# Layer 0 attention with two heads' scores in two row halves of the array and one exponential for both, and linear attention issued between groups of value products

## The chip, the cores and the metric

The kernel runs on one core of one Trainium2 chip. The metric is the time of one execution in microseconds of the device; three runs of the kernel before gave a median of 3662.07 us (3659.19 to 3665.93). The engines are named as in the profile: PE (TensorE, the matrix array; PEld are its weight loads), DVE (VectorE), ACT (ScalarE), POOL (GpSimd) and SP (SyncE, which issues most of the transfers). Each engine takes its own instructions in the order in which they were written to it, and waits on semaphores for the others. All arithmetic is in 32 bits; A matmul of F32R operands is one instruction of the array, one of plain F32 operands is two (L914 is written 592 times and stands 1184 times in the profile); products in F32R are made exact enough by splitting an operand into a high and a low part.

## What is computed

Two layers over 2048 latent tokens with 256 context tokens ahead of them, so T = 2304 rows in 18 tiles of 128. Layer 0 has two mixers side by side, latent attention (8 heads, 96 numbers in a query or key, of which 64 without and 32 with rotary positions, 64 in a value) and bidirectional gated linear attention (4 heads); layer 1 is neighbourhood attention. The part that matters here, cut from the reference:

```python
def block_attention(q, k, v, scale):
    ...
    def one(qi):
        s = jnp.einsum('bqhd,bkhd->bhqk', qi, k, preferred_element_type=jnp.float32) * scale
        p = jax.nn.softmax(s, axis=-1).astype(v.dtype)
        return jnp.einsum('bhqk,bkhd->bqhd', p, v)
    ...
def gla_scan(q, k, v, g, s0):
    ...
    def step(state, inp):
        qi, ki, vi, gi = inp
        b = jnp.cumsum(gi, axis=-2)
        b_last = b[..., -1:, :]
        q_t = qi * jnp.exp(b)
        k_t = ki * jnp.exp(-b)
        att = jnp.where(mask, jnp.einsum('bhld,bhmd->bhlm', q_t, k_t), 0.0)
        o = jnp.einsum('bhld,bhde->bhle', q_t, state) + jnp.einsum('bhlm,bhme->bhle', att, vi)
        k_dec = ki * jnp.exp(b_last - b)
        state = state * jnp.exp(b_last)[..., 0, :, None] + jnp.einsum('bhld,bhle->bhde', k_dec, vi)
        return state, o
```

Latent queries attend to all 2304 keys, context queries to the 256 context keys. The linear attention runs forward and backward over the rows, context first.

## The kernel before

The program is written with a framework that places each engine's instructions by dependencies and by the order of the text, and hoists work that is ready; `tc.issue_after(x)` adds an edge that keeps what is traced inside it behind `x` on `x`'s engine. What lies around the change:

**Latent stage** (`even_latent`). For each tile of rows `fin` turns queries and keys to one column per row, splits them into high and low and stores them to the scratch tensors `QT` and `KT`, [head, part, 97, T]: rows 0 to 95 the numbers, row 96 of the high part of `KT` ones. `even_rest` makes the remaining projections; its `maxes` takes the largest score of each row from the high parts and stores its negative as row 96 of `QT`, so that the scores come out with the maximum taken off.

**Attention** (`even_attention`). Heads go in four pairs `j`. For each pair there are five query blocks `nb`: 256 context queries against two key tiles, then four blocks of 512 latent queries against 18 key tiles. For each key tile and head three matmuls add up in one PSUM bank `st`: high keys by high queries (L972, 97 rows with the maximum), high keys by low queries (L973) and low keys by high queries (L974). ACT takes the exponential into `apt` and DVE adds it to `acc`, one instruction each per head. Value products are queued in `pend`; whenever six key tiles stand there, four are issued (`tail`, L914), each head into its own column half of one bank `av`, in plain F32. Two key tiles after a block's last value product `end` calls `finish`: column sums of `acc` into the bank `den` (L846), logarithm, exponential, the division and the gate on POOL, and the store to `RT`. PSUM holds three `st` banks, one `den`, two `av` and two `gl`.

**Linear attention** (`gla`). It is called once after the attention's first step, so its text stands ahead of nearly all of the attention's, and the framework fills in scores and values where it waits. For each of 18 chunks `front` makes the logits (L720), the logarithm of the sigmoid on ACT, cumulative sums (L731) and sums by halves (L735) and the decayed queries and keys; `back` transposes them (L758), multiplies within the chunk (L768, 64 rows each, forward and backward directions in the two row halves of the array), then by the values (L777, L783). After all chunks come two scans (forward on POOL, backward on DVE) and, in backward order, the read (L822) and write (L834). All of it shares the two `gl` banks.

**Around both** (`even_mix`). After the linear attention's text come 16 loads and splits of the output weights into places that the linear attention has left, then the remaining attention; `project` follows.

Of the kernel before, what the change touches and what calls it, by code (L numbers as in the profile page):

```python
# [17 lines left out]
P = 128  # L18
# [70 lines left out]
class Kern:  # L89
# [311 lines left out]
    def even_latent(self, ws, wrest, kept):  # L401
        nc, tc = self.nc, self.tc
        self.QT = self.scr("QT", (A_HEADS, 2, A_QK + 1, T), F32)
        self.KT = self.scr("KT", (A_HEADS, 2, A_QK + 1, T), F32)
        self.Vn = self.scr("Vn", (P, NT, 512), F32)
        self.Un = self.scr("Un", (NT, P, 1568), F32)
        with ExitStack() as es:
# [34 lines left out]
            one = self.tl(sp, [P, Q_LORA], "sql", bufs=1)  # L442
            nc.gpsimd.memset(one[:8], 1.0)
            for o in range(0, T, Q_LORA):
                nc.sync.dma_start(self.KT[:, 0, A_QK, o : o + Q_LORA], one[:8])
# [104 lines left out]
            def fin(t):  # L550
                qn, kn = nat.pop(t)
                for z, (src, dst) in enumerate(((qn, self.QT), (kn, self.KT))):
                    col = 2 * z + (0 if t < NCT else 1)
                    for h2 in range(2):
                        ps = self.tl(pp, [P, 4, P], "tp")
                        for j in range(4):
# [6 lines left out]
                        nc.sync.dma_start(  # L563
                            dst[h2 * 4 : h2 * 4 + 4, :, :A_QK, t * P : t * P + P].rearrange("h s d t -> d (h s) t"),
                            hl[:A_QK].rearrange("d h s t -> d (h s) t").bitcast(F32))
# [42 lines left out]
    def even_rest(self, ws, win, hT):  # L608
        nc = self.nc
        self.zaT = self.scr("zaT", (4, P, T), F32)  # L610
        with ExitStack() as es:
# [33 lines left out]
            def maxes():  # L645
                for h in range(A_HEADS):
                    k = self.tl(sp, [P, T], "mk", F32R, bufs=2)
                    nc.sync.dma_start(k[:A_QK].bitcast(F32), self.KT[h, 0, :A_QK])
                    m = self.tl(sp, [P, NT, 5], "mm")
                    nc.vector.memset(m[:], -3e38)  # L650
                    for t in range(NT):
                        if t % 6 == 0:
                            q = self.tl(sp, [P, 768], "mq", F32R)
                            nc.sync.dma_start(q[:A_QK].bitcast(F32), self.QT[h, 0, :A_QK, t * P : t * P + 768])
# [13 lines left out]
                    nc.gpsimd.dma_start(self.QT[h, 0, A_QK].rearrange("(t p) -> t p", p=P), r[:NT].bitcast(F32))  # L668
# [9 lines left out]
    def gla(self, gp, gs, g1, gd, pp, tag):  # L678
# [25 lines left out]
        z4 = lambda a: a.rearrange("p (h z d) -> p h z d", z=2, h=H)  # L704

        def front(c):

            u = self.tl(g1, [P, 1056], "gu")
            nc.sync.dma_start(u[:], self.Un[c, :, :1056])
            gq, gk, gv = u[:, :256], u[:, 256:512], u[:, 512:1024]  # L710
            ps = bank()
            u3 = self.tl(gs, [P, 3, 32], "gu3")
            g.tensor_copy(u3[:], u[:, 1024:1056].unsqueeze(1).to_broadcast([P, 3, 32]))
# [4 lines left out]
            yield  # L718
            lg = bank()
            nc.tensor.matmul(lg[:], r[:], gw[:], start=True, stop=True)  # L720
# [5 lines left out]
            nc.vector.scalar_tensor_tensor(out=G[:], in0=lg[:], scalar=0.0, in1=e[:], op0=ALU.min, op1=ALU.subtract)  # L726
# [62 lines left out]
        for _ in front(0):  # L789
            pass  # L790
# [68 lines left out]
    def even_attention(self, ap, pp, ahead):  # L859
# [133 lines left out]
        while late:  # L993
            step_late()
# [742 lines left out]
```

## Time and profile before

| | |
|---|---|
| median of three runs | 3662.07 us (3659.19 to 3665.93) |
| span of the profiled execution | 3650.5 us |
| PE busy | 3552.0 us, 97% |
| DVE, ACT, POOL busy | 65%, 39%, 34% |
| latent stage | about 0 to 550 us |
| layer-0 attention with linear attention | 1093 to 1974 us |
| linear attention within it | to about 1880 us |

The page gives no time of its own for the profiled execution beside its span; the span runs from the first to the last instruction. A row of a group of instructions has line, engine, operation, tile written <- tiles read, shapes and count, then the busy time in us, the mean of one in ns, and the idle time of the engine just ahead of them with what ended it. A row of the order of time has start and length in us, then the same names; like instructions in a row are merged, and what stands in brackets is idle time and its cause. A row of a table of stretches has the stretch, its length, busy time and count of each engine, the clock granted to TensorE as a share of full, and the transfers' share. A row of waits has who waited for whom, the total in us, the times and the longest. Line 106 is the helper that issues every activation.

### The profile page before, as it was taken

To read this page: it belongs to the slowest core of one execution; us is meant where nothing else is said; L and a number is where in the kernel's file an instruction comes from. 1 tells how busy PE (TensorE), PEld (TensorE's weight loads), DVE (VectorE), ACT (ScalarE), POOL (GpSimd) and SP (SyncE) were. 2 spreads that over 40 slices of the span, in tenths; PEclk is the share of its full clock that TensorE was granted. 3 is DMA by queue.
4 is the path that set the end of the run, shared out by engine and by line. 5 is a ranking of instruction groups with operands and counts; after the bars stand their busy time and mean duration, and the time that the engine had idled before them with its cause. 6 is when DMAs were issued, how large, how long until landed. Compare 5 with 4: busy or idle time off the path is not lost. (4 is left out here: it accounts for less than half of the span.)

```text
span 3650.5 us, 51811 instructions
## 1 busy us (share of the span) xinstructions
PE 3552.0 (97%) x18404; PEld 2747.6 (75%) x18404; DVE 2355.2 (65%) x4846; ACT 1433.2 (39%) x2740; POOL 1234.9 (34%) x1376
## 2 busy tenths in 40 slices
PE   8999999999999999999999999999899999999899
PEld 6988987888886666665656887888788887555577
DVE  4677666888876766678765435455488784666732
ACT  5445551111115555555654214444422222555510
POOL 1433330101011211221311224333344442888763
PEclk9999999999999999999999999999999999999999
DMA  7455463222243232342632544545734446898672
GB/s 259 142 156 155 135 177 110 87 75 84 69 116 86 66 107 66 89 125 66 179 110 93 184 139 141 159 146 155 245 126 144 131 133 181 212 223 220 190 235 97
DMA packets 365780, 512.25 MB, mean 140 GB/s; under 512 B 26081, under 2 KB 245297, under 8 KB 359618
## 3 DMA queue, kind: packets, MB, share of 16 engines
q1 hardware_dynamic: 320754, 417.69, 39.3%
q0 software_dynamic: 22112, 63.26, 5.7%
q10 hardware_dynamic: 22656, 27.99, 2.2%
q8 instruction: 146, 2.39, 0.3%
q14 instruction: 112, 0.92, 0.1%
HBM read 329.45 MB, written 179.37 MB: 139 GB/s over the span
## 5 line engine op out<-in xcount | busy, mean ns | idle before, releaser
L963 DVE TENSOR_TENSOR acc<-acc,apt 128x512 f32<-128x512 f32 x512 | 375.6, 756 | 168.5 <-ACT apt L106 165.6
L106 ACT ACTIVATE apt<-st 128x512 f32<-128x512 f32 (+1 forms) x592 | 343.6, 594 | 290.7 <-PE st L974 262.0
L660 DVE TENSOR_REDUCE mm<-mx 128x1 f32<-128x512 f32 (+1 forms) x656 | 388.7, 629 | 87.3 <-PE mx L659 80.0
L914 PE MATMUL av<-apt,av 128*64 128x512 f32 (+1 forms) x1184 | 280.6, 594 | 0.0
L972 PE MATMUL st<-aq,akh 97*128 97x512 f32 (+1 forms) x592 | 256.6, 434 | 8.8 <-DMA aq<-QT 4.4
L659 PE MATMUL mx<-mk,mq 96*128 96x512 f32 (+1 forms) x656 | 235.8, 373 | 5.0 <-DMA mq<-QT 3.4
L1430 POOL TENSOR_TENSOR oacc<-oacc,opt 128x576 f32<-128x576 f32 (+5 forms) x192 | 223.0, 1184 | 39.7 <-ACT rl L106 19.3
L973 PE MATMUL st<-aq,akh 96*128 96x512 f32 (+1 forms) x592 | 235.5, 398 | 0.0
L1548 DVE TENSOR_TENSOR opt<-st,tab 128x64 f32<-128x64 f32 (+10 forms) x576 | 144.6, 317 | 140.3 <-PE st L1391 63.8
L974 PE MATMUL st<-aq,akl 96*128 96x512 f32 (+1 forms) x592 | 234.4, 396 | 0.0
L106 ACT ACTIVATE u<-gm 128x352 f32<-128x352 f32 (+1 forms) x140 | 68.6, 498 | 373.2 <-PE gm L131 210.6
L1307 DVE CUSTOM_DVE_ANT_1 mx<-mx,mtab 128x217 f32<-128x217 f32 (+12 forms) x576 | 184.2, 338 | 40.1 <-PE mx L1301 30.9
L914 PEld LDWEIGHTS av<-apt,av 128*64 128x64 f32 x1184 | 80.5, 137 | 153.6 <-issue 152.3
L972 PEld LDWEIGHTS st<-aq,akh 97*128 97x128 f32 x592 | 113.0, 191 | 99.1 <-issue 50.5
L106 ACT ACTIVATE opt<-opt 128x930 f32<-128x930 f32 (+7 forms) x129 | 104.2, 810 | 110.7 <-DVE opt L1548 102.6
L659 PEld LDWEIGHTS mx<-mk,mq 96*128 96x128 f32 x656 | 121.2, 188 | 16.8 <-DMA mk<-KT 3.8
L974 PEld LDWEIGHTS st<-aq,akl 96*128 96x128 f32 x592 | 113.9, 193 | 25.6
L973 PEld LDWEIGHTS st<-aq,akh 96*128 96x128 f32 x592 | 114.4, 193 | 17.1
L129 PE MATMUL gm<-w1h,hhi 128*128 128x512 f32 x288 | 116.3, 404 | 6.8 <-ACT onat L106 6.8
L106 ACT ACTIVATE x<-px,modB,modA 128x128 f32<-128x128 f32 x272 | 99.3, 468 | 56.9 <-PE px L339 54.4
L129 PE MATMUL gm<-w0h,hhi 128*128 128x512 f32 x288 | 116.3, 404 | 2.0 <-DVE hhi L351 1.9
L807 POOL TENSOR_TENSOR gsf<-gsf,D 64x512 f32<-64x512 f32 x17 | 25.1, 1477 | 271.4 <-DVE D L784 271.4
(492 smaller groups left out, 9962.1 us busy)
## 6 DMA issues: line engine op xcount, KB each, us to landing
q<-Q SPq DMA_DIRECT2D x48, 512.0 KB
H<-x ACTq DMA_DIRECT2D x36, 512.0 KB
adaw<-ada_w SPq DMA_DIRECT2D x64, 256.0 KB
x<-H SPq DMA_DIRECT2D x32, 512.0 KB
wraw<-w_od SPq DMA_DIRECT2D x64, 256.0 KB
K1t<-okt POOLq DMA_DIRECT2D x32, 512.0 KB, 7.6
kt<-K1t SPq DMA_DIRECT2D x32, 512.0 KB
mtab<-rpb_q SPq DMA_DIRECT2D x16, 899.0 KB
```

The costliest lines, as they stand in the source:

```text
L106: return self.nc.scalar.activation(out, in_, func, **kw)
L129: self.nc.tensor.matmul(out, lh(k), rh(k), start=j == 0, stop=False)
L659: mm = nc.tensor.matmul(ps[:, :w], q[:A_QK, (t % 6) * P : (t % 6) * P + P], k[:A_QK, k0 : k0 + w], start=True, stop=True)
L660: nc.vector.tensor_reduce(out=m[:, t, n : n + 1], in_=ps[:, :w], axis=AX.X, op=ALU.max)
L914: nc.tensor.matmul(O[j, nb][i * 64 : i * 64 + 64, :w], V[j, kt // TT][:, kt % TT, i * 64 : i * 64 + 64], pts[i][:, :w], start=n == 0, stop ...
L963: nc.vector.tensor_tensor(out=acc[i][:, :w], in0=a[:, :w], in1=pts[i][:, :w], op=ALU.add)
L972: nc.tensor.matmul(ps[:, :w], kh[: A_QK + 1, i, kq], qh[: A_QK + 1, :w], start=True, stop=False)
L973: nc.tensor.matmul(ps[:, :w], kh[:A_QK, i, kq], ql[:A_QK, :w], start=False, stop=False)
L974: mm = nc.tensor.matmul(ps[:, :w], kl[:A_QK, i, kq], qh[:A_QK, :w], start=False, stop=True)
L1307: nc.vector.tensor_tensor_reduce(out=s, in0=s, in1=tb[:, ri : ri + rn, ci : ci + cn], scale=1.0, scalar=-3e38, op0=ALU.add, op1=ALU.max, a ...
L1430: self.psum = nc.gpsimd.tensor_tensor(out=a, in0=a, in1=pts[:, :, a0 - r0 : a1 - r0, :], op=ALU.add)
L1548: bias = nc.vector.tensor_tensor(out=pt[:, d[0], d[1]], in0=ps[:, d[0], d[1]], in1=tabs[j][i][:, ri : ri + rn, ci : ci + cn], op=ALU.add)
```

## The change

Scores of two heads are made together. A score is split into 64 plain and 32 rotary numbers: scratch tensors are now `QA`, `KA` ([part, head, 64, T]), `QC`, `KC` ([head, part, 32, T]) and `QM` (the negative maxima). A key tile of a head pair has slot 0 with 64 plain numbers of one head in rows 0 to 63 and of the other in 64 to 127, and slot 1 with the rotary numbers (high ones twice in the high tile; the low ones with a row of ones in the low tile). Five terms take the place of three, each a matmul of one head in rows 0 to 63 and of the other in 64 to 127 of the array: plain high by high, high by low and low by high; rotary high keys by high and low queries at once; rotary low keys by high queries with the ones by the negative maximum (33 rows). They go to a `st` of two banks, of which there are two; one activation and one addition cover both heads. `den` is taken from the `gl` banks.

The linear attention becomes a generator of 128 steps (`low_rank`, `logits`, `decays`, `turn`, `within`, `values`, `scan`, `read`, `write`), followed by 16 steps of output weights. Where four value products are issued, one step is drawn ahead of them, behind the scores, and one behind them. The first two query blocks of the next head pair are loaded at the third key tile of the block before.

```diff
-        self.QT = self.scr("QT", (A_HEADS, 2, A_QK + 1, T), F32)
-        self.KT = self.scr("KT", (A_HEADS, 2, A_QK + 1, T), F32)
+        self.QA, self.KA = [self.scr(n, (2, A_HEADS, A_NOPE, T), F32) for n in ("QA", "KA")]
+        self.QC, self.KC = [self.scr(n, (A_HEADS, 2, A_ROPE, T), F32) for n in ("QC", "KC")]
+        self.QM = self.scr("QM", (A_HEADS, T), F32)
...
-                        nc.sync.dma_start(
-                            dst[h2 * 4 : h2 * 4 + 4, :, :A_QK, t * P : t * P + P].rearrange("h s d t -> d (h s) t"),
-                            hl[:A_QK].rearrange("d h s t -> d (h s) t").bitcast(F32))
+                        hs, ts = slice(h2 * 4, h2 * 4 + 4), slice(t * P, t * P + P)
+                        for part in range(2):
+                            nc.sync.dma_start(da[part, hs, :, ts].rearrange("h d t -> d h t"), hl[:A_NOPE, :, part, :].bitcast(F32))
+                        nc.sync.dma_start(dc[hs, :, :, ts].rearrange("h s d t -> d (h s) t"),
+                                          hl[A_NOPE:A_QK].rearrange("d h s t -> d (h s) t").bitcast(F32))
...
+        def scan(c, sl, eng, name):
...
+        low_rank(0)
+        yield
+        low_rank(1)
+        logits(0)
+        yield
+        for c in range(NT):
+            decays(c)
+            yield
+            if c + 2 < NT:
+                low_rank(c + 2)
+            if c + 1 < NT:
+                logits(c + 1)
+            yield
+            turn(c)
+            yield
+            within(c)
+            yield
+            values(c)
+            scan(c, slice(0, 64), nc.gpsimd, "gsf")
+            yield
+        order = self.back_order()
+        for n in range(NT + 1):
+            if n < NT:
+                scan(order[n], slice(64, 128), nc.vector, "gsb")
+                read(order[n])
+                yield
+            if n:
+                write(order[n - 1])
+                yield
...
+            for part in range(2):
+                dma(q[:, part, :w], self.QA[part, 2 * j : 2 * j + 2, :, qs].rearrange("h d t -> (h d) t"))
+            dma(q[:, 2, :w], self.QC[2 * j : 2 * j + 2, :, :, qs].rearrange("h s d t -> (h s d) t"))
+            for i in range(2):
+                dma(q[i * 64 : i * 64 + 32, 3, :w], self.QC[2 * j + i, 0, :, qs])
+            for i in range(2):
+                last = dma(q[i * 64 + 32 : i * 64 + 33, 3, :w], self.QM[2 * j + i : 2 * j + i + 1, qs])
...
-            self.finish(O.pop((j, nb))[:, :w], sums.pop((j, nb)), zt[:, :w], self.RT[j, :, q0 : q0 + w], w, ap, pp, ("den", 1))
+            self.finish(O.pop((j, nb))[:, :w], sums.pop((j, nb)), zt[:, :w], self.RT[j, :, q0 : q0 + w], w, ap, pp, ("gl", 2))
...
-                        ps = self.tl(pp, [P, 512], "st", bufs=3)
-                        nc.tensor.matmul(ps[:, :w], kh[: A_QK + 1, i, kq], qh[: A_QK + 1, :w], start=True, stop=False)
-                        nc.tensor.matmul(ps[:, :w], kh[:A_QK, i, kq], ql[:A_QK, :w], start=False, stop=False)
-                        mm = nc.tensor.matmul(ps[:, :w], kl[:A_QK, i, kq], qh[:A_QK, :w], start=False, stop=True)
-                        pt = self.tl(ap, [P, 512], "apt", bufs=14)
-                        self.act(pt[:, :w], ps[:, :w], AF.Exp, scale=A_SCALE)
+                    ps = self.tl(pp, [P, 2, 512], "st", bufs=2)
+                    terms = ((kh, 0, 0, 64), (kh, 0, 1, 64), (kl, 0, 0, 64), (kh, 1, 2, 64), (kl, 1, 3, 33))
+                    for m, (k, kb, qb, r) in enumerate(terms):
+                        for o in (0, 64):
+                            mm = nc.tensor.matmul(ps[:, o // 64, :w], k[o : o + r, kb, kq], Q[o : o + r, qb, :w], start=m == 0, stop=m == 4)
+                    pts = self.tl(ap, [P, 2, 512], "apt", bufs=7)
+                    self.act(pts[:, :, :w], ps[:, :, :w], AF.Exp, scale=A_SCALE)
...
                     with self.tc.issue_after(mm.ins):
                         step_late()
                         if len(pend) == 6:
+                            next(side, None)
                             for _ in range(4):
-                                tail(*pend.pop(0))
+                                mm = tail(*pend.pop(0))
+                            with self.tc.issue_after(mm.ins):
+                                next(side, None)
+                    if nb == 4 and j < 3:
+                        if n == 2:
+                            for b in range(2):
+                                early[b], _ = queries(j + 1, b)
```

240 lines of the change are left out of this document (123 added, 117 removed).

## The prediction

> **What bounds the kernel now.** I read the page's first lines, then the table of stretches for the layer-0 attention, then the groups of instructions in it.
>
> ```profile
> span 3650.5 us, 51811 instructions
> PE 3552.0 (97%) x18404; PEld 2747.6 (75%) x18404; DVE 2355.2 (65%) x4846; ACT 1433.2 (39%) x2740; POOL 1234.9 (34%) x1376
> core 0: us, PE busy (x) PEld busy (x) DVE busy (x) ACT busy (x) POOL busy (x), PEclk, DMA share, GB/s
> 1095.00:1975.00 880.00, 868.17 (x4223) 537.66 (x4224) 607.04 (x879) 479.42 (x957) 168.83 (x167) 0.99 0.33 93
> L914 PE MATMUL av<-apt,av 128*64 128x512 f32 x1152 | 276.2, 600 | 0.0
> L972 PE MATMUL st<-aq,akh 97*128 97x512 f32 x576 | 251.3, 436 | 7.5 <-DMA aq<-QT 4.4 <-ACT apt L106 3.0
> L973 PE MATMUL st<-aq,akh 96*128 96x512 f32 x576 | 231.1, 401 | 0.0
> L974 PE MATMUL st<-aq,akl 96*128 96x512 f32 x576 | 230.2, 400 | 0.0
> ```
>
> PE sets the end: 868 of 880 us in this stage. ACT and DVE are busy 54% and 69% of it. So only PE time, or a new PE wait, counts. A matmul's listed duration (0.40 us) overlaps its neighbours; its price is the distance from its start to the next start. I read that from the order of time near the end of the stage, where the linear attention is finished and only scores (L972 to L974) and value products (L914) run.
>
> ```profile
> 1903.42 0.40 PE L973 MATMUL st<-aq,akh 96*128 96x512 f32 x1
> 1903.42 0.19 PEld L974 LDWEIGHTS st<-aq,akl 96*128 96x128 f32 x1
> 1903.65 0.40 PE L974 MATMUL st<-aq,akl 96*128 96x512 f32 x1
> 1903.98 3.65 PE L914 MATMUL av<-apt,av 128*64 128x512 f32 x16
> 1904.89 0.14 PEld L914 LDWEIGHTS av<-apt,av 128*64 128x64 f32 x2 [0.29 <-issue]
> 1905.32 0.14 PEld L914 LDWEIGHTS av<-apt,av 128*64 128x64 f32 x2 [0.29 <-issue]
> 1907.56 0.50 PE L972 MATMUL st<-aq,akh 97*128 97x512 f32 x1
> 1907.90 0.39 PE L973 MATMUL st<-aq,akh 96*128 96x512 f32 x1
> 1908.14 0.40 PE L974 MATMUL st<-aq,akl 96*128 96x512 f32 x1
> 1908.37 0.40 PE L972 MATMUL st<-aq,akh 97*128 97x512 f32 x1
> 1908.57 5.50 ACT L106 ACTIVATE apt<-st 128x512 f32<-128x512 f32 x8 [3.88 <-PE st L974]
> 1913.04 0.40 PE L974 MATMUL st<-aq,akl 96*128 96x512 f32 x1
> 1913.37 3.65 PE L914 MATMUL av<-apt,av 128*64 128x512 f32 x16
> ```
>
> From 1908.37 to 1913.04 there are 20 steps: a score matmul costs 0.2335 us. Value products start in pairs (two column halves, loaded "x2") every 0.43 us. A cycle of four key tiles runs from 1903.98 to 1913.37, 9.39 us: 24 x 0.2335 = 5.60 for scores, 8 x 0.43 = 3.44 for values, and 0.35 left for going over between whole array and column halves and back: about 0.10 at each border (1903.65 to 1903.98 is 0.33, 1907.56 to 1907.90 is 0.34, against 0.2335) and the rest at the neighbours, so **0.17 us a change of tiling**.
>
> **The sum, part by part.** *Scores.* A head's three matmuls of 96 or 97 rows become, for two heads, five pairs of at most 64 rows. There are 4 x 4 x 18 = 288 pairs of tiles of 512 queries (and 8 of 256). Everything hangs on whether two row halves run at once. The stage has such matmuls, in the linear attention (L768):
>
> ```profile
> 1147.55 0.50 PE L768 MATMUL gl<-gqT,gkT 64*128 64x128 f32 x6
> 1147.67 0.31 PEld L768 LDWEIGHTS gl<-gqT,gkT 64*128 64x128 f32 x4
> 1152.87 0.50 PE L777 MATMUL gl<-gu,gat 128*128 128x128 f32 x3
> ```
>
> In the same 0.50 us six half-array matmuls pass, or three whole ones, of the same 128 columns; four weight loads pass in 0.31 us though one takes 0.19. So halves do run, and load, side by side, and the second costs nothing. Hence a pair at the price of one: 5 x 0.2335 = 1.17 us where 6 x 0.2335 = 1.40 stood, 0.234 x 288 = **-67 us**, and -1 for the 8 narrow tiles. The bounds: a pair may go as fast as half of a value pair, 0.215 (0.43 / 2), which gives -94; or both halves may share something that L768 doesn't load fully (its plain-f32 columns go no faster than one per 0.43/512 us, the new ones go at twice that), up to no gain at all from pairing, 10 x 0.2335, +269 us. I take the side that L768 shows.
>
> *Changes of tiling.* Before, most linear attention ran in whole-array form next to whole-array scores, free of a change. Now scores are in halves, values in column halves, and each of 128 side steps (2 + 18 x 5 + 18 x 2 by the code) sits at one of 146 places, before or after the value products of 73 cycles. Each such step adds one change, except the 18 of `within`, which have the scores' own form: 110 x 0.2 = 22 us (0.17, rounded up for the smaller matmuls). Against it, the old `within` and the score tiles cut through by it gave some 43 changes, 9 us. Net **+13**; bounds 0 and +25.
>
> *Exponentials.* One exponential for both heads; its source is two PSUM banks, and `st` has two buffers in place of three.
>
> ```profile
> L106 ACT ACTIVATE apt<-st 128x512 f32<-128x512 f32 x576 | 338.0, 600 | 283.3 <-PE st L974 254.5 <-PE av L914 2.6
> L106 ACT ACTIVATE apt<-st 128x256 f32<-128x256 f32 x16 | 5.7, 390 | 7.5 <-PE st L974 7.4
> L106 ACT ACTIVATE hhi<-x 128x1024 fp32r<-128x1024 f32 x32 | 33.9, 1058 | 44.0 <-PE gm L130 43.7
> L963 DVE TENSOR_TENSOR acc<-acc,apt 128x512 f32<-128x512 f32 x512 | 375.6, 756 | 168.5 <-ACT apt L106 165.6
> L365 DVE TENSOR_TENSOR hlo<-x,hhi 128x1024 fp32r<-128x1024 f32 x32 | 42.2, 1319 | 12.2 <-ACT hhi L106 12.2
> ```
>
> 600 and 390 ns extrapolate to 1.02 us, and 1058 is near it; ACT and DVE get lighter (1.02 for 1.20, 1.32 for 1.51), which is worth nothing under PE. But in a group of four tiles the third must wait for the first's exponential: scores end at 1.17, the exponential starts 0.2 later (1908.14 + 0.2335 to 1908.57), ends at 2.39, while the second tile's scores end at 2.34. With a handover of 0.1 that is 0.15 us; the fourth then just fits. 73 x 0.15 = **+11**. If each exponential stands behind one 0.6 us linear-attention activation, 73 x 0.6 = +44; if handover is free, 0.
>
> *Linear attention at fixed places.* PE takes its queue in order, and the change writes the order out: a step whose operands are late now holds the scores or value products behind it, where before other scores filled in.
>
> ```profile
> 1125.55 0.39 PE L720 MATMUL gl<-gw,rT 98*128 98x512 f32 x1
> 1130.19 0.60 PE L731 MATMUL gl<-gG,tri 128*128 128x256 f32 x2
> ```
>
> From the logits (L720) to the decays that need them (L731) lie 4.64 us in the first chunk: three activations, a DVE operation and the queues. From a step before the values to the one after them there are 3.44 + 0.35 = 3.8 us, from one behind the values to the next 4 x 1.17 + 0.35 = 5.0. So logits fall short by 0.85 us when they stand before the values, in half of 18 chunks: 8 us; the chains `decays` to `turn` and `within` to `values` have two DVE operations and the group's last exponential before them, and I give them as much together: **+16**; bounds 0 and 128 x 0.75 = +96.
>
> *Denominators* move into the linear attention's two banks (its own bank goes to `st`). A bank is held over two activations and a DVE operation, 0.6 + 0.6 + 0.7 and handovers, some 2.3 us, and is taken two score tiles (2.3 us) ahead of the next side step: 20 x 0.25 = **+5**, 0 to +20.
>
> *Loads.* The next heads' first two query blocks are asked for at the third tile of the block before.
>
> ```profile
> PE st L972 <- DMA aq<-QT: 4.4, 2, 2.3
> 1290.00:1390.00 100.00, 97.67 (x488) 62.04 (x485) 59.17 (x85) 50.03 (x104) 21.47 (x22) 0.97 0.39 109
> 1690.00:1790.00 100.00, 94.92 (x450) 59.55 (x449) 70.11 (x107) 55.59 (x121) 25.99 (x26) 0.97 0.59 160
> L563 SPq DMA_DIRECT2D QT<-qkhl x36: 304/327/339, 104.0 to 540.7; - x36
> 100.00:200.00 100.00, 98.83 (x602) 91.41 (x601) 66.95 (x122) 53.07 (x131) 39.46 (x74) 1.00 0.49 142
> 1056.15 0.38 SPq L877 DMA_DIRECT2D akh<-KT  x1
> L972 PE MATMUL st<-aq,akh x592: 281/396/795, 1093.6 to 1970.4; 97*128 97x512 f32 x192, 97*128 97x256 f32 x6
> ```
>
> Both 2.2 us waits go, and, I take it, half of the clock loss in the two stretches (0.03 x 100 each): **-7**; 0 if another wait takes their place. In the latent stage 72 stores become 216, 144 x 0.33 = 48 us of SyncE's issue over 445 us in front of a PE that is 98.8% busy, and the input loads queue behind them. Key loads grow from one to five issues of 0.38 us, low parts to three, queries to seven; all start 37 us ahead of the first score. Without that cover the first blocks' eleven more would cost 4 us. I put **+1**, up to +6. The removed memset and three stores of ones, and the twice-split loads of the maxima, hide behind the same PE work: 0.
>
> Sum: -67 - 1 + 13 + 11 + 16 + 5 - 7 + 1 = **-29 us**. The profile's span is 3650.5; the runs' median, 3662.07, has 11.6 us around it, which the change doesn't touch: 3633.
>
> **Rivals.** *(a) The waits win, slower.* The mechanism of the side steps with its upper bound: each of 128 steps waits 0.75 us on average, +96 in place of +16: **3713**. It decides from (29 + 16) / 128 = 0.35 us a step. For it: chains of three to five ACT and DVE operations, with two banks for all of them; POOL's part waits too. Against it: most gaps are longer than the shortest distance above, and the scheduler may hoist the DVE and ACT parts.
>
> *(b) Everything fits:* pairs at 0.215 and no waits: -94 - 1 + 13 - 7 + 1 = -88, **3574**.
>
> *(c) A wash:* waits of 0.35 us a step, **3662**.
>
> *(d) Halves only partly side by side* at the new rate: with a pair midway between 0.2335 and 0.467, 0.35, scores cost 1.75 in place of 1.40, +101 in place of -67: **3801**; with nothing side by side 3969. The whole sum turns at (1.40 - 38 / 288) / 5 = 0.254 us a pair. For it: no row here loads both halves at the full column rate. Against it: L768.
>
> [...]
>
> *(e) Weights not loaded ahead:* if a load to one row half had to wait for that half's matmul to end, a pair would cost its 0.2335 and the 0.10 that an uncovered load costs at a border today, 0.334: (5 x 0.334 - 1.40) x 288 = +78 in place of -67: **3778**. The row at 1903.42 speaks against: the load for L974 starts with the matmul of L973 on the same rows.
>
> [...]
>
> **How the numbers follow.** Likeliest: 3633, chance 0.46, own range 3600 to 3655. (a) 0.20, (b) 0.15, (c) 0.08, (d) 0.07, (e) 0.04. The range takes in (b) and (a): 3574 to 3713; outside it stand (d), (e) and the ends of (a) and (b). About 0.2%, 7 us, is what a measurement of this kernel can tell from no change. Faster than that: the likeliest and (b), 0.61; within it (c), 0.08; slower (a), (d), (e), 0.31.
>
> **What would show it.** In the changed profile: score matmuls starting in pairs at 0.23 to 0.24 us (0.25 or more speaks for (d) or (e)); the third tile of each group released by ACT after a short wait; side steps waiting for ACT or DVE, 0.1 to 0.3 us on average if I am right, over 0.4 if (a) is; about 0.75 us of changes in a cycle with two steps; no wait for `aq` at the second block of a head pair; a latent stage of the same length. A clock below 0.95 in the stage, or a wait of PE at the end of the stage for the output weights, would be something that I left out.

## The result, and the profile after

The changed kernel takes 3670.36 us (median of 8 runs), the kernel before 3659.77 beside it: ratio 1.0035, 95% interval 1.0024 to 1.0045. It is slower by 13 us, where 29 us faster was forecast. The head of the changed kernel's page:

```profile
span 3666.0 us, 53771 instructions
PE 3536.1 (96%) x19588; PEld 2703.1 (74%) x19588; DVE 2317.0 (63%) x4570; ACT 1401.2 (38%) x2444; POOL 1251.8 (34%) x1377
```

Its layer-0 attention as before, and the crowded part of it, when the linear attention is read out; behind it the kernel before at its own most crowded part (stretch, length, busy us of each engine with instructions, then the granted clock):

```profile
core 0: us, PE busy (x) PEld busy (x) DVE busy (x) ACT busy (x) POOL busy (x), PEclk, DMA share, GB/s
1095.00:1975.00 880.00, 839.27 (x5352) 486.16 (x5353) 565.51 (x598) 443.44 (x656) 194.70 (x171) 0.97 0.33 100
1670.00:1755.00 85.00, 65.79 (x372) 38.95 (x368) 80.87 (x96) 35.11 (x55) 30.45 (x21) 0.86 0.38 107
```

```profile
1610.00:1700.00 90.00, 85.29 (x369) 50.54 (x367) 85.65 (x123) 43.70 (x78) 12.13 (x9) 0.96 0.25 72
```

The costliest groups of the changed kernel's stage beside the products:

```profile
L1029 DVE TENSOR_TENSOR acc<-acc,apt 128x1024 f32<-128x1024 f32 x256 | 336.4, 1314 | 158.9 <-ACT apt L106 146.2
L106 ACT ACTIVATE apt<-st 128x1024 f32<-128x1024 f32 x288 | 292.4, 1023 | 204.0 <-PE st L1022 186.8 <-PE av L971 4.9 <-DVE D L802 2.0
```

PE is less busy than before (839 us of 880, against 868) and yet ends later. VectorE is 95% busy in the crowded part of either kernel, but PE is 95% busy beside it before and 77% after, at a granted clock of 0.86. The exponential at 1023 ns and the sum at 1314 ns are what was predicted (1.02 and 1.32 us). The longest waits of the stage from 1098 us on that bear on the scores, first before, then after (engine and line, what it waited for, us in total, count, longest):

```profile
PEld st L972 <- ACT apt L106: 18.2, 22, 2.8
PE st L972 <- ACT apt L106: 3.0, 2, 2.3
ACT ge L106 <- DVE goi L823: 1.5, 1, 1.5
```

```profile
PEld st L1022 <- ACT apt L106: 57.8, 65, 5.4
ACT ge L106 <- DVE goi L831: 53.0, 14, 7.7
PE st L1022 <- ACT apt L106: 32.0, 17, 5.0
```

The waits for queries (`aq`) are gone, as predicted. In their place scores wait for a buffer that an exponential must free (`st` for `apt`), and the square of the linear attention's reads (`ge`) waits for VectorE's sum `goi`.

The next table was worked out from the start times of the recorded products: each product's time runs to the start of the next, summed by kind, from the 12th to the 240th key tile's value products, in us. "Changes" counts neighbours of different tiling; "alone" counts value products of the whole stage with no other starting within 0.09 us, so with no partner in the other column half. A wait counts for the product ahead of it: 8 of the 22 us of the changed kernel's denominators are waits of the scores behind them. The lower rows are experiments that follow.

| kernel | scores | values | linear att. | denom. | sum | changes | alone |
|---|---|---|---|---|---|---|---|
| before | 360 | 213 | 120 | 14 | 707 | 214 | 48 |
| after | 334 | 219 | 141 | 22 | 716 | 341 | 74 |
| e12, old scores, nothing beside | 344 | 207 | - | 14 | 565 | 146 | 8 |
| e11, row halves, nothing beside | 289 | 202 | - | 14 | 505 | 146 | 8 |
| f5, old scores, pieces kept whole | 365 | 202 | 124 | 15 | 706 | 196 | 0 |
| f4, row halves, pieces kept whole | 304 | 206 | 149 | 17 | 676 | 299 | 0 |

Scores fell by 26 us in this stretch where 228 x 0.234 = 53 were forecast, and every other kind rose.

A second sum from the same start times is for the whole stage and sets *gaps* apart: a step of more than 0.53 us from one start to the next counts as a gap with all that it has over the usual 0.2335 us (in us; the last column, time at half clock, lies within the others).

| kernel | scores | values | linear att. | denom. | gaps | stage | half clock |
|---|---|---|---|---|---|---|---|
| before | 448 | 273 | 126 | 18 | 15 | 879 | 20.5 |
| after | 392 | 277 | 151 | 18 | 50 | 887 | 47.8 |
| f1, change with pairs kept | 385 | 263 | 149 | 16 | 52 | 866 | 34.1 |
| f5, old scores, pieces kept whole | 447 | 262 | 128 | 17 | 24 | 877 | 27.3 |
| f4, row halves, pieces kept whole | 374 | 258 | 147 | 17 | 51 | 847 | 34.1 |

### The profile page after: what moved, and what is told of

Its sections match the earlier page's. It is cut to its first block, busy times and chain, and to the rows that moved or that the text cites. A ratio compares the mean times of both kernels' runs of the same rounds, so it can differ in the third digit from the quotient of the medians.

```text
span 3666.0 us, 53771 instructions
## 1 busy us (share of the span) xinstructions
PE 3536.1 (96%) x19588; PEld 2703.1 (74%) x19588; DVE 2317.0 (63%) x4570; ACT 1401.2 (38%) x2444; POOL 1251.8 (34%) x1377
## 5 line engine op out<-in xcount | busy, mean ns | idle before, releaser
L1029 DVE TENSOR_TENSOR acc<-acc,apt 128x1024 f32<-128x1024 f32 x256 | 336.4, 1314 | 158.9 <-ACT apt L106 146.2
L106 ACT ACTIVATE apt<-st 128x1024 f32<-128x1024 f32 (+1 forms) x296 | 296.8, 1011 | 209.7 <-PE st L1022 192.6
L1022 PE MATMUL st<-aq,akh 64*128 64x512 f32 x1728 | 333.6, 426 | 31.5 <-ACT apt L106 31.4
L971 PE MATMUL av<-apt,av 128*64 128x512 f32 (+1 forms) x1184 | 288.2, 596 | 3.0 <-DVE rc L895 3.0
L1022 PEld LDWEIGHTS st<-aq,akh 64*128 64x128 f32 x1728 | 164.1, 192 | 136.4 <-ACT apt L106 57.1
L1022 PE MATMUL st<-aq,akl 64*128 64x512 f32 (+1 forms) x1152 | 247.7, 406 | 0.0
L1022 PEld LDWEIGHTS st<-aq,akl 64*128 64x128 f32 (+1 forms) x1152 | 122.1, 192 | 27.7 <-issue 2.0
L210 POOL TENSOR_TENSOR oss<-oss,mhalf 128x8 f32<-128x8 f32 x68 | 112.8, 1659 | 5.1
L130 PE MATMUL gm<-w1l,hhi 128*128 128x512 f32 x288 | 114.5, 398 | 0.0
L130 PE MATMUL gm<-w0l,hhi 128*128 128x512 f32 x288 | 114.2, 397 | 0.0
```

Of the source, the lines that this page charges most:

```text
L106: return self.nc.scalar.activation(out, in_, func, **kw)
L130: self.nc.tensor.matmul(out, lh(k), rl(k), start=False, stop=False)
L210: g.tensor_tensor(out=out, in0=out, in1=self.mhalf[:, : shp[1]], op=ALU.pow)
L971: mm = nc.tensor.matmul(O[j, nb][i * 64 : i * 64 + 64, :w], V[j, kt // TT][:, kt % TT, i * 64 : i * 64 + 64], pts[:, i, :w], start=n == 0, ...
L1022: mm = nc.tensor.matmul(ps[:, o // 64, :w], k[o : o + r, kb, kq], Q[o : o + r, qb, :w], start=m == 0, stop=m == 4)
L1029: nc.vector.tensor_tensor(out=acc[:, :, :w], in0=a[:, :, :w], in1=pts[:, :, :w], op=ALU.add)
```

## The experiments

Times are ratios to the kernel before, run beside them; 0.001 is 3.7 us. The edits are abridged. The expectations name theories by letters: A is waiting behind exponentials that stand in ScalarE's queue; B is changes of tiling in e1 to e3, and a full VectorE from e5 on; C and D are said where they come up.

| kernel | what it is | ratio [95%] |
|---|---|---|
| e1 | change, linear attention's text ahead of attention | 1.0466 [1.0451, 1.0482] |
| e2 | order of the change, old scores | 0.9970 [0.9957, 0.9983] |
| e3 | change, paced backward scan | 1.0025 [1.0015, 1.0036] |
| e4 | change, latent stores in one transfer | 1.0050 [1.0033, 1.0066] |
| e5 | change, late square, a third `goi` buffer | 1.0026 [1.0014, 1.0037] |
| e6 | e5 with the paced scan | 0.9989 [0.9979, 1.0000] |
| e7 | change, two exponentials | 1.0041 [1.0027, 1.0054] |
| e8 | e2, late square, paced scan | 0.9979 [0.9967, 0.9990] |
| e9 | e6, square behind the exponentials | 1.0105 [1.0084, 1.0126] |
| e10 | e8, square behind the exponentials | 1.0003 [0.9992, 1.0013] |
| e11 | row halves, linear attention after 19 blocks | 1.0501 [1.0483, 1.0520] |
| e12 | old scores, linear attention after 19 blocks | 1.0666 [1.0644, 1.0688] |
| f1 | change, pairs kept | 0.9986 [0.9976, 0.9997] |
| f2 | e6, pairs kept | 0.9939 [0.9926, 0.9952] |
| f3 | e8, value pairs kept | 0.9962 [0.9950, 0.9974] |
| f4 | f2, tiles and groups kept whole | 0.9909 [0.9894, 0.9923] |
| f5 | old scores in f4's order | 0.9981 [0.9972, 0.9989] |
| f6 | f1, tiles and groups kept whole | 0.9955 [0.9941, 0.9968] |

**Undoing one half of the change each (e1, e2).** e1 drains the linear attention before the first block, e2 puts the steps around value products into the kernel before.

```
 e1:  att = self.even_attention(ap, pp, split, iter(())); next(att)
      for _ in more: pass          # then the blocks of att
 e2:  old scores, old buffers and `den`; gla() in steps, next(side) before and after tail x4
```

> The changed kernel with the linear attention's text ahead of the attention's again, so only the pairing, the one exponential and the new loads are left. Theory A (the loss is waiting: in the stretch of the reads DVE is the bound, the scores' exponentials stand in ACT's queue behind linear-attention activations, and PE waits for a score buffer): with free filling the waits shrink, 3630 to 3650 us, 10 to 30 under before. Theory B (the loss is changes of tiling: linear attention in whole-array form among half-array scores): it is cut in more often, so no faster than the changed kernel, 3665 us or more.

> The kernel before with only the linear attention as steps around the value products; scores, three score banks and the denominator's own bank as before. Theory A: the same waits in the stretch of the reads, but with exponentials of 0.6 us and three banks; 5 to 30 us over before. Theory B: whole-array scores need no further changes, so within 7 us of before.

The two halves don't add as expected. The order alone is 11 us faster, so the row halves and what goes with them cost 0.0065, 24 us, in that same order. In e1 the scores hardly ran while the linear attention did (the value products of key tiles 12 to 24 took from 1145 to 1553 us; from 1193 to 1590 us PE was busy for 252 of 397 us at a granted clock of 0.63), so its time says little of the scores; why they stood still there was not settled.

**Two side causes (e3, e4).** e3 spreads the backward scan over the reads instead of letting it run ahead in VectorE's queue; e4 stores the latent queries and keys as before, in one transfer, and splits the loads.

```
 e3: +  for n in range(4): back(n)
     +  with self.tc.issue_after(self.added.ins): back(n + 3)   # added: last sum of exponentials
 e4: -  three stores into QA/KA, QC/KC      +  one store into QS/KS, loads by head
```

> The changed kernel with the backward scan of a chunk kept behind the additions of its own step, three chunks ahead of the read, in place of all at once. Theory A: DVE falls from 95% to about 80% in the first 85 us of the reads, the 3 to 5 us waits of scores on ACT go there, and with them half-clock time; 20 to 30 us under the changed kernel, 3640 to 3650. Theory B: within 7 us of the changed kernel.

> The changed kernel with queries and keys of the latent stage stored by one transfer a tile again (plain and rotary numbers in one scratch tensor, loads in the attention split more). If the three stores cost the 5 us by which the attention starts later (1098.8 for 1093.6), the first score starts at about 1094 and the time falls by 4 to 6 us; the rival is that the later start is no effect of the stores, and then it stays within 2 us.

e3 brought 4 us, far from what theory A asked for. VectorE did fall, from 95% to 86% busy in 1670 to 1755 us, but the gaps of the stage stayed (49 us for 50): they only moved to later reads. e4 missed: its first score comes 2.7 us earlier than the change's, but the value products of its first twelve key tiles end 7.1 us later. Its loads are split further; that these are the reason was not shown.

**The queue of the exponentials (e5, e6, e8).** This is where the changed kernel stands in its crowded stretch (start, duration, engine, operation; idle time in brackets; rows of weight loads and some others left out):

```profile
1715.01 0.40 PE L1022 MATMUL st<-aq,akl 33*128 33x512 f32 x2
1715.32 0.69 DVE L815 TENSOR_TENSOR gsb<-gsb,fac 64x512 f32<-64x512 f32 x1
1716.04 0.69 DVE L831 TENSOR_TENSOR goi<-gl,goi 128x512 f32<-128x512 f32 x1
1716.76 0.69 DVE L816 TENSOR_TENSOR gsb<-gsb,D 64x512 f32<-64x512 f32 x1
1716.76 0.63 ACT L106 ACTIVATE ge<-goi 128x512 f32<-128x512 f32 x1 [7.30 <-DVE goi L831]
1717.30 1.92 ACT L106 ACTIVATE apt<-st 128x1024 f32<-128x1024 f32 x2
1718.36 1.22 PE L1022 MATMUL st<-aq,akh 64*128 64x512 f32 x4 [2.95 <-ACT apt L106]
1719.38 0.63 PE L1022 MATMUL st<-aq,akl 64*128 64x512 f32 x2
1719.80 0.63 PE L1022 MATMUL st<-aq,akh 64*128 64x512 f32 x2
1720.23 0.63 PE L1022 MATMUL st<-aq,akl 33*128 33x512 f32 x2
```

ScalarE stands 7.3 us at the square, because VectorE, at work on a scan (L815, L816), makes the sum late; two exponentials wait behind it, and PE 2.95 us behind them. Then the pairs start 0.43 us apart for a while instead of 0.23: the granted clock is 0.50 from 1718.2 to 1721.6. So the square was issued one cycle later (with a third buffer for `goi`, which holds the sum longer):

```
 +  for n in range(NT + 2):
 +      if 0 < n <= NT: norm(order[n - 1])      # square, mean, root, products
        if n < NT: read(order[n]); yield        # product with the state, sum
        if n > 1: write(order[n - 2]); yield
```

> The change, but the part of a read of linear attention from its square on (square, mean, root, two products) is issued with the next chunk's read, one cycle of four key tiles (about 9 us) later, so that the exponentials no longer stand in ACT's queue behind a square whose sum VectorE hasn't made yet. Theory A, the loss of 30 us between 1626 and 1755 us is that queue: the waits for score buffers (33 us of gaps between 1594 and 1894) fall to under 12 us, the half-clock time from 48 us to near 25, and the time to 3635 to 3652. Theory B, VectorE itself is full there and the wait only moves to the sums of the denominators: 3660 to 3675, the gaps stay over 25 us.

> The kernel of the late square, and the scan that runs backward is spread over the reads, three chunks ahead of its read, instead of running ahead in VectorE's queue. Theory A: 3630 to 3648, no more than a few us below the late square alone. Theory B, VectorE's load in 1670 to 1755 us (95% busy): this one brings more than the late square alone, by 10 us or more, since it alone thins that stretch out.

> The scores of before (three products over all rows, one exponential a head, three buffers), linear attention as steps around the value products, with the late square and the paced backward scan. Theory A: the 10 us of score waits that the order alone had in 1694 to 1794 us go, and the time is 3630 to 3642. Theory B: within 4 us of the order alone (3642 to 3650).

e5 alone gave 3 us, inside the intervals; e6 with the paced scan gave 17 us against the change (1.0035 to 0.9989), about 13 more than the late square alone, which theory B asked for. Late square and paced scan bring 3 and 4 us each alone, so the two belong together. In e6's trace gaps are 37 us for 50 and time at half clock 17 us for 48. e8 is no better than e2 (0.9979 and 0.9970), a miss for theory A. But in the recorded order the square had gone ahead of older exponentials again, so theory A wasn't tested yet.

**The square made to stand behind (e9, e10).**

```
 +  with self.tc.issue_after(self.expd.ins): norm(order[n - 1])   # expd: newest exponential
```

> The change with the late square and the paced backward scan, and the square now kept behind the newest exponential in ACT's queue (in the two kernels of the late square it had gone ahead of older exponentials again, and still waited 58 us in 18 pieces for VectorE's sum). Theory A (exponentials queued behind the square are the wait in the reads): the waits of the square for the sum fall under 15 us, the score waits between 1594 and 1894 us from 26 us to under 12, and the time is 10 to 18 us below the 0.9989 of before that the paced late square gave: 3632 to 3642 where before is 3654. Theory B, VectorE is the bound there: no more than 4 us below it, the wait goes to the sums of the denominators.

> The same three edits on the scores of before. Theory A: the score waits between 1594 and 1894 us (15 us) halve, and the time is 4 to 10 us below the 0.9979 of the late square there. Theory B: within 3 us of it.

Theory A falls: e9 is 0.0116 slower than e6, 42 us, and e10 0.0024 slower than e8, 9 us, where both were to be faster. Waits of the attention in e6, then in e9:

```profile
ACT ge L106 <- DVE goi L831: 58.1, 18, 6.2
PE st L1034 <- ACT apt L106: 23.7, 17, 5.3
```

```profile
PEld st L1035 <- ACT apt L106: 76.9, 69, 7.0
PE st L1035 <- ACT apt L106: 48.5, 25, 6.5
ACT gsf L106 <- POOL goi L844: 39.3, 14, 6.9
```

The square no longer waits, but what depends on it is later: ScalarE now stands at the next link, `gsf`, for POOL's product. The wait belongs to the chain of a read across four engines, not to its square. A full VectorE alone isn't the cause either: from 1670 to 1755 us it is 95% busy in the change, 90% in e6 and 76% in e9, and e9 is the slowest of the three. What in e6's two edits does it together was not taken apart.

**The exponential (e7).**

```
 -  ps = self.tl(pp, [P, 2, 512], "st", bufs=2)          +  two of [P, 512], bufs=4
 -  self.act(pts[:, :, :w], ps[:, :, :w], AF.Exp)        +  one for each head
```

> The change, but with one exponential of 128x512 for each head and four score buffers of one bank in place of two of two banks. ScalarE gets 288 x (two of about 0.58 us less one of 1.01 us) = about 43 us more work. Theory A, the exponentials wait behind linear attention and not for the size of a buffer: the same waits, and some more, 3665 to 3690. Rival, the coarse buffers (a bank pair comes free only once both heads are through) make PE wait: the gaps at scores fall by 15 us or more and the time is 3640 to 3658.

It comes out 0.0006 above the change, inside both intervals. Its score waits are smaller than the change's (PE 19.1 us for 32.0), against theory A's expectation, and the gaps of the stage are 39 us for 50. But its order is another one: with two separate banks 1047 of the 2960 score products start with no other within 0.09 us, for 62 in the change, and the scores take 416 us of the stage for 392. So it doesn't show by itself what the two-bank buffers cost.

**Row halves with nothing beside them (e11, e12).** Both run the first 19 blocks of attention with no linear attention in PE's queue.

```
 -  self.even_attention(ap, pp, split, more)     +  self.even_attention(ap, pp, split, iter(()))
 +  behind the value products of block 19:  for _ in more: pass
```

> The change, with all of linear attention and the output weights issued behind the value products of the 19th of 20 blocks, so that the first 19 run with nothing beside them. Slower as a whole (linear attention's chain then stands bare for some hundreds of us); read against the kernel with the old scores in the same order. Theory C (the row halves save what was predicted, and mixing linear attention in between gives it back by changes of tiling and waits): from the first value product to the 240th key tile 0.23 to 0.26 us a key tile less than the old scores, 55 to 62 us. Rival (the saving is lost in the attention itself: exponentials, buffers, denominators): under 35 us.

> The scores of before, with all of linear attention and the output weights issued behind the value products of the 19th block. The first 19 blocks at 2.44 to 2.48 us a key tile under Theory C (292 key tiles of three products twice, one pair of value products and a change of tiling to and fro each four), against 2.18 to 2.24 us for the row halves; under the rival both within 0.12 us.

From the 12th to the 276th key tile e12 takes 652.4 us (1130.8 to 1783.2) and e11 585.6 (1144.1 to 1729.7): 66.8 over 264 tiles, **0.253 a tile**. (Theory C: the row halves save what was predicted, and mixing linear attention in gives it back.) The first 12 tiles are left out: in e11 an exponential waits there 10 us behind a copy of the gate weights that come late. Value groups of e12, then a stretch of e11:

```profile
1169.56 3.65 PE L955 MATMUL av<-apt,av 128*64 128x512 f32 x16
1178.94 3.65 PE L955 MATMUL av<-apt,av 128*64 128x512 f32 x16
```

```profile
1507.67 3.65 PE L971 MATMUL av<-apt,av 128*64 128x512 f32 x16
...
1511.82 0.40 PE L1023 MATMUL st<-aq,akl 64*128 64x512 f32 x2
1512.05 0.40 PE L1023 MATMUL st<-aq,akh 64*128 64x512 f32 x2
1512.29 0.39 PE L1023 MATMUL st<-aq,akl 33*128 33x512 f32 x2
1512.52 0.62 PE L1023 MATMUL st<-aq,akh 64*128 64x512 f32 x4
...
1513.43 0.39 PE L1023 MATMUL st<-aq,akl 33*128 33x512 f32 x2
1513.80 0.73 PE L1023 MATMUL st<-aq,akh 64*128 64x512 f32 x4
...
1516.33 3.65 PE L971 MATMUL av<-apt,av 128*64 128x512 f32 x16
```

Pairs ("x2") start 0.23 us apart. A cycle of four tiles is 8.66 us for 9.38, so 0.18 a tile; the third tile starts 0.37 after the last pair in place of 0.23, the short wait that was predicted (0.15). The rest is waits of e12 for `aq` (9.9 us in 3) and half-clock time (20.5 us, none in e11), so that 0.253 fell into the 0.23 to 0.26 of theory C partly by chance; 0.18 is the figure to hold against the forecast, 0.19 with the exponentials' wait taken off. Theory C holds: the loss is in the mixing.

**Pairs cut in two (f1, f2, f3).** The next rows are the changed kernel's PE in the middle of a value group, and then the kernel before at such a place:

```profile
1380.97 0.66 PE L767 MATMUL gl<-ident,gqt 128*128 128x128 f32 x4
1381.56 3.65 PE L971 MATMUL av<-apt,av 128*64 128x512 f32 x14
1385.14 0.66 PE L767 MATMUL gl<-ident,gkt 128*128 128x128 f32 x4
1385.72 1.07 PE L971 MATMUL av<-apt,av 128*64 128x512 f32 x2
1386.72 0.74 PE L1022 MATMUL st<-aq,akh 64*128 64x512 f32 x4
```

```profile
1182.04 3.65 PE L914 MATMUL av<-apt,av 128*64 128x512 f32 x14
1185.61 1.13 PE L731 MATMUL gl<-gG,tri 128*128 128x256 f32 x4
1186.67 1.07 PE L914 MATMUL av<-apt,av 128*64 128x512 f32 x2
```

A whole group is 16 products in 3.58 us. Here 14 take the same 3.58 (1381.56 to 1385.14), and the other two 1.00 more. The last tile's left column half ran alone, then four transposes came, then its right half alone. The planner that lays out PE's queue takes what it believes ready, and doesn't know that two halves are cheap only as neighbours. By the order of the starts, value products have 20 such cuts in the changed kernel, 12 in the kernel before and 4 in e2; 23 more go through pairs of scores in the changed kernel, where the old scores have no pairs to cut. Theory D takes these for the loss. f1 binds the second half to the first:

```
 +  with self.tc.issue_after(first.ins), self.tc.high_priority():
        mm = nc.tensor.matmul(... second half ...)      # values and scores
```

> The change, with the second half of every pair of value products and of every pair of scores put right behind the first in PE's queue, so that no linear attention can stand between two halves; nothing else. Theory D (the loss is pairs that the order cuts in two: in the changed kernel 74 value products and 62 score products start alone, against 8 and 3 where linear attention doesn't run beside them): 66 x 0.215 + 59 x 0.117 = 21 us less than the changed kernel's 1.0035 of before, so 3640 to 3652 where before is 3655. Rival, the halves that ran alone only filled time in which PE would have waited: 3660 or more.

> The kernel with the late square and the paced backward scan (0.9989 of before), with the pairs kept together. If the two losses, cut pairs and VectorE's crowd in the reads, are separate, the 21 us come off this too: 3625 to 3638. If the pairs' gain is eaten by waits for VectorE in the reads: 3642 or more.

> A control: the scores of before with linear attention in the order of the change, the late square and the paced scan (0.9979 of before; 16 value products alone), with the halves of the value products kept together. Theory D: 8 x 0.215 = 2 us less, within 4 us of it, 3643 to 3651.

Theory D holds: f1 is 0.0049 under the change, 18 us for 21 expected, and f2 takes 18 us off e6 as well. The trace shows it where it should be: values take 14 us less than in the change and scores 7 less, as expected, while the gaps stay (52 us for 50). The control moved 6 us where 2 were expected; its interval and that of e8 overlap.

**Tiles and groups kept whole (f4, f5, f6).** All ten score products of a tile, and all products of four value tiles, are chained in the same way.

```
 f4, f6: +  mm = mm if m else None     # the ten of a tile
         +  mm = tail(*pend.pop(0), mm)       # the group of four
```

> As the paced kernel with kept pairs, and besides all ten score products of a key tile, and all products of a group of four value tiles, without anything between them: 75 pieces of value products in place of 91 and some 20 fewer pieces of linear attention. Theory: some 40 fewer changes of tiling at 0.1 to 0.2 us, 4 to 8 us below the paced kernel with kept pairs. Rival, steps that could fill waits no longer can: the same or up to 10 us above.

> The scores of before in the best order: linear attention around the value products, late square, paced scan, the three score products of both heads of a key tile and each group of value products kept together. Against the row halves in the same order (0.9909 of before) this is what the row halves themselves are worth. If the order was all that kept the 67 us away: this one at 0.996 to 1.000, the row halves 20 us or more ahead. If row halves are worth little beside linear attention in any order: 0.989 to 0.994.

> The change with scores of a key tile and groups of value products kept together, without the late square and the paced scan: what keeping them together brings by itself. The kept pairs alone gave 0.9986 and kept pairs with pacing 0.9939, so pacing is worth 17 us there; if the two add up as before, 0.9909 + 0.0047, 3640 where before is 3657; if fewer cuts also relieve VectorE's stretch, under 3632.

f4 runs in **3622.86 us**, ratio 0.9909: faster than both kernels. Fewer pieces brought 11 us (f2 to f4; f1 to f6 the same), more than the 4 to 8 expected; in the traces the products take 12 and 14 us less, but the gaps are 7 and 12 us more, so how the 11 come about isn't settled. f6 also shows that pacing and whole pieces add (0.9955, where 0.9956 was expected). f5 answers the last question: in the same order row halves are worth 0.9981 - 0.9909 = 0.0072, 26 us. For f4, its stage and its crowded tiles, then its waits for score buffers:

```profile
1095.00:1946.00 851.00, 813.08 (x5418) 479.35 (x5417) 577.30 (x603) 448.72 (x661) 197.49 (x169) 0.98 0.34 103
1640.00:1720.00 80.00, 74.21 (x470) 42.80 (x472) 69.27 (x78) 40.67 (x60) 29.32 (x22) 0.96 0.48 147
```

```profile
PEld st L1046 <- ACT apt L106: 34.0, 35, 4.1
PE st L1046 <- ACT apt L106: 20.5, 15, 3.7
```

PE is 93% busy in the crowded tiles (77% in the change), at a granted clock of 0.96 (0.86).

## Why the prediction was wrong

With the gaps set apart, the sum can be held against the stage. Products were to take 44 us less (-67 - 1 + 13, and + 11, since the third tile's short wait is too small to be a gap) and took 27 less. Gaps were to be 17 more (16 + 5, less the 4 of `aq`) and are 35 more. The clock was to give 3 and the latent stage to cost 1; the stage starts 5 later. So the two misses are of one size: 17 us in the products and 18 in the gaps.

- **Scores, -67: right.** A pair costs 0.23 us in e11, and attention by itself gains 0.18 us a key tile once `aq` waits and half clock are taken out; the sum, with the 11 us of the exponentials in it, had 0.19. Rivals (d) and (e), at 0.35 and 0.334 us a pair, are out.
- **Changes of tiling, +13: the step that failed.** It said that each step "adds one change", so it took a step as one piece and the pairs as uncut. Steps come in several pieces: 341 changes for 214 in 228 key tiles, 127 more where the sum had 110 less 43 in the whole stage. The price held, the count did not: gaps apart, linear attention takes 21 us more in these tiles, 0.17 a change, and 25 in the whole stage. Above all, pieces stand between halves: 20 pairs of value products and 23 of scores are cut. That has no term in the sum; keeping pairs gave 18 us, keeping tiles and groups whole 11 more. Part of the 18 is not new, since the kernel before has 12 cuts too: by the prices of f1's expectation (0.215 us for a value product alone, 0.117 for a score) the change added about 13, an estimate. The rows of the prediction came from the end of the stage, where no linear attention runs, and so couldn't show the cuts that the kernel before had already.
- **Linear attention at fixed places, +16: right in kind, too small.** Gaps are 50 us in the stage, 15 before, so 35 more, 0.27 a step, inside the bound of 96 that stood for rival (a). They aren't spread over 128 steps, as (a) had it: most stand in the reads, where VectorE is 95% busy. Time at half clock rose from 20.5 us to 47.8, worth 14 us more, which lies within the gaps and the products; the sum had it fall by 3 us. Why the kernel before gets through as full a VectorE with PE at 95% was not tried; late square and paced scan together (e6, f2) recover 17 us of it.
- **Exponentials, +11: right where nothing runs beside.** The short wait of the third tile is there (0.37 us for 0.23 in e11). With linear attention mixed in, scores wait for two-bank buffers (PE 32.0 us in the change), and e7 doesn't settle how much of that is their size.
- **Denominators, +5: not seen by themselves.** From their starts to the next start it is 29.8 us, 18.5 before, but these 11 us are three waits behind them in which scores stood for `st`, and are counted with the gaps. Without them the products take 17.7 us, 17.5 before.
- **Loads, -7: half right.** The two waits for `aq` (4.4 us) went, the clock didn't improve (0.97 of full over the stage, 0.99 before). The first value product comes 8.7 us later than before. Of these 5.2 are the later first score; the other 3.5 went while half the clock was granted (0.50 in 1100.4 to 1110.0 us), for e6 and f1, with the same loads, take 8.4 us from the first score to the first value product, like the kernel before (8.7).
- **Latent stage, +1:** +5 in this profile, inside the bound of 6. That the stores cause it isn't shown: f3 has the old ones and starts its scores at 1098.3, as late as the change (1098.8). The stores that the sum counted over 445 us lie in 437 (104.0 to 540.7), which changes nothing.

By the number, rival (c), a wash by waits of 0.35 us a step, comes nearest; by the mechanism it has only half, the waits; the other half of the miss lies in the products.

That f4 is 33 us under the kernel before, where 29 were predicted, is in part luck: its values take 15 us less than before, since it lacks the cuts that the kernel before has, and its gaps are 36 us more. By the ratios, cut pairs cost 18 us, the pieces within tiles and groups 11, the reads 17; together 46 between f4 and the change. In f4's order row halves are worth 26 us of the 67: against f5, f4's scores take 73 us less and its values 3, but linear attention takes 19 more, with 103 more changes of tiling, and gaps are 27 more.

## What to carry to other kernels

The saving from two products side by side was here a property of neighbours in the queue: pieces between halves cut 20 pairs of value products and 23 of scores, and keeping the pairs gave 18 us (f1). So read the issue order, and count the halves that start alone, before pricing such a saving, and bind the halves together if a planner lays the order out. Price a new tiling in the stretch where other work is mixed in, not where it runs bare: whole-array pieces that were free beside whole-array products (in the kernel before they start 0.23 us after a score, as another score does) paid a change beside halves (0.33 us after a score in the change; 0.17 us a change by the sum over 228 key tiles). When a wait sits in a chain across engines, moving one link of it in a queue may only move the wait (e9, 42 us slower than e6), and thinning out the fullest engine alone may bring little (e3, 4 us); here only both edits together helped (e6, 17 us).

## What was not expected of the hardware

- The two row halves of the array ran fully side by side at 512 columns, over long stretches: in e11 the pairs start 0.23 us apart (1511.82, 1512.05, 1512.29), no slower than one whole-array product of the kernel before (0.2335), where rival (d) had 0.35.
- Half clock came with the end of a PE wait of 2.95 us (the wait ends at 1718.36; granted clock 0.50 from 1718.2 to 1721.6, pairs 0.43 us apart from 1719.38 on). The time at half clock in the stage is a multiple of 3.41 us: 20.5 us, 6 times that, before, and 47.8 us, 14 times, after. In both traces the stretches at half clock start whole multiples of 3.41 us apart over the whole span; in the change five of them start at 1684.02, 1701.09, 1718.16, 1735.22 and 1752.29, 5 times 3.41 us from one to the next. What sets these starts was not shown.
